# The value tiles of an mLSTM projection: 640 tokens with x stationary, and a written order of the first loads

## The chip, the core and the metric

The kernel runs on one core of one Trainium2 chip, in one launch. The time is device time in microseconds (us), the median of several runs. The engines are named as in the profile: PE is TensorE's matmuls and PEld its weight loads, DVE is VectorE, ACT is ScalarE, POOL is GpSimd, SP is SyncE, which issues most DMAs. "L1360" is line 1360 of the kernel before.

## The reference

One step of a hybrid decoder layer on 1024 prompt tokens and 8 decode tokens, 1032 rows in all, of width 2048. RMSNorm, then one projection of every token, whose columns feed two groups of heads:

```python
(aq, ak, av, iq, ik, iw, az, mq, mk, mv, mi, mf, mo, mz) = jnp.split(h @ w_in, split_points, axis=-1)
```

- Sparse attention (8 query heads, 2 key heads): an indexer (iq, ik, iw) scores all keys, the best 256 are kept, and attention runs over these. The decode tokens do the same over a paged cache of 4096 positions.
- An mLSTM with 4 heads (mq, mk of 128 a head, **mv of 256 a head**, gates mi, mf), run over the prompt in chunks, with its matrix state C returned.

Both are gated (az, mo, mz), joined, multiplied with w_out and added to x; a last RMSNorm follows. Outputs are y for prompt and sample, the new keys and values, and the mLSTM states. The change bears on `mv`, 1024 of the projection's columns, and on the first 70 us.

## The kernel before, in words

**Number format.** Every matmul operand is split in two: H, its rounded part, and L, the rest. A product is H·xH + H·xL + L·xH, three matmuls. x times the norm's weight is held in SBUF as `xH[k]` and `xL[k]`, 16 k-tiles of 128 rows x 1032 tokens. The norm's 1/rms is a factor per token, applied when a result leaves PSUM.

**The projection** is 61 tiles `t` of 128 columns. Weights are stationary, tokens move in three chunks of 344 (two of 388, from token 256 on, for the indexer's queries), and the result has columns on partitions and tokens along the free axis. `proj` (L1363) runs a tile in 4 quarters of 4 k-tiles; per quarter one DMA of 256 KB brings the raw weights (`wload`, `wsplit`, L190 to L220), ACT casts them to `wH` (L213) and DVE subtracts to get `wL` (L214). There are 2 raw buffers and 3 of H and L each. `mm` issues the matmuls (L1360). `evac` multiplies with `rstd`, tokens along the free axis, on DVE (L333), and writes the result to SBUF or by DMA to a scratch tensor in HBM. Tile order: misc (0), iq (1 to 8), ak and av (9 to 12), aq (13 to 20), mq, mk, mv (21 to 36, **mv is 29 to 36**), gates mo, mz (37 to 52), az (53 to 60).

**PSUM** has 8 banks: `pj0` to `pj2` for the projection, and five of a rotating `bank` for the rest.

**The work beside the projection.** The projection is the bed into which all else is laid. Two `Lane`s hold lists of `Job`s (from L1313): generators that do a piece of work and yield its weight. After each quarter, `lane.step(now)` lets each lane run as many pieces as the job's due tile asks for. Lane 0 has gates, index (indexer scores and a bit search for the 256th best), att, ml (the mLSTM); lane 1 has dscore (gathers from the paged cache and scores of the decode tokens), dsel, datt and dml. `gates`, `index` and `dscore` start with tile 9. A scheduler then orders each engine's queue by priority; `high_priority()` marks loads and evacuations, and `pin` fixes instructions in the order in which they are written.

**mLSTM.** `evac` writes q, k and v of the mLSTM to `mlS` (`mlS<-ev` in the DMA groups). `job_ml` later fetches one chunk of 128 tokens and one pair of heads per step, 16 steps, and in its preparation (L818 to L835) transposes the four 128 x 128 blocks of v on PE (L826) so that tokens lie on partitions, and copies them out of PSUM to `aH` (L833).

**The start.** `xbegin` (L269) loads the first k-tile of x in three pieces with the first weights; `xload` (L294) loads each further k-tile whole (516 KB), splits it on ACT (L265) and DVE (L266), squares it on ACT and adds the squares into `acc` on DVE. Tiles 0, 1 and 2 run together while x arrives, in seven PSUM banks (three for tile 0, two for each of the others). After their last matmul `row_rstd` (L233) sums `acc` over the partitions on PE (L239), takes the power -1/2 on POOL (L248), and turns the result with nine transposes (L255) and copies on DVE (L257) into `rstd`; then the three tiles are evacuated.

**The output projection** uses two forms: 392 tokens with weights stationary (L1487), and 640 tokens with the activations stationary and 512 columns of weights moving (L1525).

Of the kernel before, what the change touches and what calls it, by code (L numbers as in the profile page):

```python
# [41 lines left out]
T_AK = 9  # L42
T_AV = 11
T_AQ = 13
T_MQ = 21
T_MK = 25
T_MV = 29
# [18 lines left out]
def column_order():  # L66
    off = np.cumsum([0, 1024, 256, 256, 1024, 64, 16, 1024, 512, 512, 1024, 4, 4, 1024, 1024])
    aq, ak, av, iq, ik, iw, az, mq, mk, mv, mi, mf, mo, mz = off[:14]
    misc = np.concatenate([np.arange(ik, ik + 64), np.arange(iw, iw + 16),
                           np.arange(mi, mi + 4), np.arange(mf, mf + 4)])  # L70
    cols = [iq + np.arange(1024), ak + np.arange(256), av + np.arange(256),
            aq + np.arange(1024), mq + np.arange(512), mk + np.arange(512), mv + np.arange(1024)]
# [3 lines left out]
    return misc, np.concatenate(cols)  # L76
# [22 lines left out]
class Lane:  # L99
# [26 lines left out]
    def step(self, now):  # L126
        self.now = now
        self.debt -= 1.0
# [12 lines left out]
def body(tc, A, stop=None):  # L141
# [32 lines left out]
    cntp = ear.tile([128, 2, NB], F32, name="cntp")  # L174
    mhalf = fix.tile([128, 1], F32, name="mhalf")
# [57 lines left out]
    def row_rstd(accs, out, n, pool):  # L233
        m = (n + 127) // 128
        p = bank()
        for c in range(m):
            w = min(128, n - c * 128)
            for x, acc in enumerate(accs):
                PE.matmul(p[:w, c:c + 1], acc[:, c * 128:c * 128 + w], onesf[:, 0:1],  # L239
                          start=(x == 0), stop=(x == len(accs) - 1))  # L240
        r = pool.tile([128, 16], F32, name="rr", bufs=1)
        V.memset(r, 1.0)
        f = n // 128
        V.tensor_scalar(r[:, :f], p[:, :f], 1.0 / D, EPS, OP.mult, OP.add)
        if f < m:
            w = n - f * 128
            V.tensor_scalar(r[:w, f:m], p[:w, f:m], 1.0 / D, EPS, OP.mult, OP.add)
        G.tensor_tensor(r[:, :m], r[:, :m], mhalf.to_broadcast([128, m]), OP.pow)  # L248
        yield
        for c4 in range(0, m, 4):  # L250
            p = bank()
            n4 = min(512, n - c4 * 128)
            for c in range(c4, min(m, c4 + 4)):
                w = min(128, n - c * 128)
                PE.transpose(p[:, (c - c4) * 128:(c - c4) * 128 + w], r[:w, c:c + 1].to_broadcast([w, 128]),  # L255
                             ident[:w, :w])
            V.tensor_copy(out[:, c4 * 128:c4 * 128 + n4], p[:, :n4])  # L257
            yield
# [10 lines left out]
    def xbegin():  # L269
# [21 lines left out]
        pin(SC.activation(acc, xr, AF.Square))  # L291
        return [w[:2] for w in ws]

    def xload(k):  # L294
# [5 lines left out]
        sq = x0.tile([128, R], F32, name="sq", bufs=2)  # L300
        SC.activation(sq, xr, AF.Square)
        V.tensor_tensor(acc, acc, sq, OP.add)
# [3 lines left out]
    def chunks(t):  # L306
        return CHQ if T_IQ <= t < T_AK else CH

# [10 lines left out]
    def evac(t, ps, cols, pool=None, norms=None):  # L319
# [3 lines left out]
        for c, (c0, cn) in enumerate(chs):  # L323
            if full is not None:
                e = full[:cols, c0:c0 + cn]
            elif t < T_AK:
# [3 lines left out]
            if T_MK <= t < T_MV:  # L330
# [8 lines left out]
            elif t < T_AK:  # L339
# [23 lines left out]
            elif t < T_G:  # L363
                j = t - T_MQ
                hp, slot = ((j // 2, j % 2), (j // 2 - 2, 2 + j % 2), (j // 4 - 2, 4 + j % 4))[min(j // 4, 2)]
# [175 lines left out]
    def job_att():  # L541
        early.close()
# [235 lines left out]
    def job_ml():  # L778
        gT = mlc["gT"]
        with tc.tile_pool(name="ml", bufs=2) as pm:  # L780
# [37 lines left out]
            def prep(c, h0, qk, vT, dk, d, qt):  # L818
# [5 lines left out]
                pv = bank().rearrange("p (a b) -> p a b", a=2)  # L824
                for x in range(4):
                    PE.transpose(pv[:, x // 2, (x % 2) * 128:(x % 2) * 128 + 128], vT[:, x, :], ident)  # L826
# [100 lines left out]
    def job_dscore():  # L927
        with tc.tile_pool(name="ds", bufs=2, side="right") as pd:
# [29 lines left out]
            for b in range(NB):  # L958
                bd = pd.tile([128, 4, 8, 16], F32, name="bd")
                pin(V.tensor_tensor(bd, iqr[:, :, :, b].unsqueeze(2).to_broadcast([128, 4, 8, 16]),  # L960
                                    g8.unsqueeze(1).unsqueeze(3).to_broadcast([128, 4, 8, 16]), OP.mult))
                ps = bank()
                for c in range(4):
                    fetch(b * 4 + c + 2)
                    yield 4
# [340 lines left out]
    def ix_weight(blocks):  # L1306
# [5 lines left out]

    lanes = [Lane([Job("gates", T_AK, T_AK + 1.5, 8500, job_gates),  # L1313
                   Job("index", T_AK, 35.5, 3000 + sum(map(ix_weight, groups)), lambda: job_index(groups)),
                   Job("att", T_MQ, 47.75, 2 * 2 * sum(2 * (1 + (i + 1) * 0.5) for i in range(8)) + 6, job_att, att_free),
                   Job("ml", T_G + 11.25, T_PRE, 38, job_ml)]),
             Lane([Job("dscore", T_AK, 18, 16 + 128 + 2, job_dscore),
                   Job("dsel", T_AK, 34, 2000 + 31 * 1700 + 10000 + 16 * 2800 + 2000, job_dsel),
# [33 lines left out]
    def wsrc(t, q):  # L1352
        return A["wm"][q] if t == 0 else A["wa"][t - 1, q]

    def mm(ps, cols, t, q, c, H, L):
        c0, cn = chunks(t)[c]
        for k in range(4):
            kk = q * 4 + k
            for w_, x_, z in ((H, xH, 0), (H, xL, 1), (L, xH, 2)):
                PE.matmul(ps[:cols, :cn], w_[:, k, :cols], x_[kk][:, c0:c0 + cn],  # L1360
                          start=(kk == 0 and z == 0), stop=(kk == 15 and z == 2))

    def proj(ts, hook=None):  # L1363
# [7 lines left out]
        for q in range(4):  # L1371
            ws = []
            for x, t in enumerate(ts):
                cols = NMISC if t == 0 else 128
                with tc.high_priority():
# [4 lines left out]
                    elif x:  # L1380
                        ws.append(wsplit(wsrc(t, q), cols, x0, 2, 4, q == 1))
                    else:
                        ws.append(wsplit(wsrc(t, q), cols, wst, 2, 3))
            for x, t in enumerate(ts):
# [12 lines left out]

    pend = []
    mids = []

    def xhook(q, ws):
        if q:
            ws.append(wsplit(wsrc(0, q), NMISC, wst, 2, 3, q == 1))
        else:
            ws += xbegin()
        for k in range(max(1, q * 4), q * 4 + 4):
            xload(k)
            if k == 2:
                SY.dma_start(cst, A["cst"][:, :NCST])
                with tc.tile_pool(name="c0", bufs=1) as c0p:  # L1410
                    ctmp = c0p.tile([128, 256], F32, name="ctmp")
                    SY.dma_start(ctmp, A["cst"][:, C_TRI:C_TRI + 256])
                    V.tensor_copy(trib, ctmp[:, :128])
                    V.tensor_copy(cmask[:, 128:256], ctmp[:, 128:256])

    pss = proj((0, 1, 2), xhook)
    with tc.high_priority():
        for _ in row_rstd([acc], rstd, R, x0):
            pass
    x0ctx.close()  # L1420
    with tc.tile_pool(name="mp", bufs=1) as mp, tc.tile_pool(name="iqp", bufs=1) as iqp:
# [5 lines left out]
        for t in range(3, T_AK):  # L1427
# [3 lines left out]
            if t == 3:  # L1431
                index_weights(misc)
    for t in range(T_AK, NT):
# [24 lines left out]
    def finish(ys, accs):  # L1458
        c0, cn = CB[0]
        rs = pb.tile([128, cn], F32, name="rs", bufs=1)  # L1460
        rr = row_rstd(accs, rs, cn, pb)
# [127 lines left out]
def layout(x_prompt, x_sample, cache_k, cache_v, cache_idx_k, state_C, state_n, state_m, page_table,  # L1589
# [6 lines left out]
    misc, cols = column_order()  # L1596
    a["wm"] = w[:, misc].reshape(4, 4, 128, NMISC).transpose(0, 2, 1, 3)
    a["wa"] = w[:, cols].reshape(4, 4, 128, NT - 1, 128).transpose(3, 0, 2, 1, 4)
# [60 lines left out]
```

## Time and profile before

| | |
|---|---|
| median of 3 runs | 2039.86 us (2039.61 to 2044.28) |
| the profiled execution | 2039.7 us, of which its span is 2037.9 |
| granted clock of PE, mean | 0.998 |
| busy: PE, PEld | 99%, 96% of the span |
| busy: DVE, ACT, POOL | 58%, 38%, 12% |
| DMA | 257.08 MB, 126 GB/s on the mean |
| loads of projection weights after tile 0 (`wraw<-in_wa_dram`) | 238 of 256 KB |
| writes of mq, mk, mv (`mlS<-ev`) | 48 of 128 KB and smaller ones |

A row of a group reads: line, engine, operation, out<-in, shape, how many, then busy us in all and mean ns of one, then idle time of the engine just before it with what ended that. A row of the timeline reads start, duration, engine, line, operation and count, in brackets the idle time before and its releaser. A row of the chain reads start, length and the run of work. A window row reads window, length, busy us (instructions) of PE, PEld, DVE, ACT and POOL, PE's granted clock, the DMA share and GB/s. Matmuls are pipelined: one starts before the records let the one before end.

### The profile page before, as it was taken

The numbers are of one execution on the slowest core, as the hardware profiler recorded it, in microseconds if no ns is written. First come the engines' busy times: TensorE is split into PE (matmuls) and PEld (weight loads), VectorE is DVE, ScalarE is ACT, GpSimd is POOL, SyncE is SP. The second block draws the span as 40 slices with busy tenths as digits, with TensorE's granted clock in tenths as the row PEclk, the third lists the DMA queues.
The fourth block names the chain that finished last, engine by engine and source line by source line (L and its number), as shares of the span: only waits on it lengthen the run. The fifth ranks groups of instructions, "written<-read, shape, count | busy, mean of one in ns | idle before, by whom it ended". The sixth has DMA issues, their size and how long they took to land.

```text
span 2037.9 us, 34353 instructions
## 1 busy us (share of the span) xinstructions
PE 2022.5 (99%) x12678; PEld 1950.9 (96%) x12678; DVE 1182.2 (58%) x2956; ACT 777.7 (38%) x1631; POOL 235.2 (12%) x294
## 2 busy tenths in 40 slices
PE   9999999999999999999999999999999999999998
PEld 8999999999999999999999999999999999998886
DVE  8333367665696876878354554446677466664331
ACT  8121234233631446312255554534444344433222
POOL 0000111100000000023211011012222211111110
PEclk9999999999999999999999999999999999999999
DMA  7444533322222212244323332146675558566212
GB/s 247 106 112 125 154 111 114 100 84 63 76 75 70 75 56 63 64 142 154 120 70 92 110 95 86 48 131 197 207 217 176 152 184 314 174 223 221 81 49 103
DMA packets 203669, 257.08 MB, mean 126 GB/s; under 512 B 39685, under 2 KB 130885, under 8 KB 203501
## 3 DMA queue, kind: packets, MB, share of 16 engines
q1 hardware_dynamic: 198253, 240.82, 38.1%
q0 software_dynamic: 4096, 12.59, 2.0%
q8 instruction: 99, 1.62, 0.3%
q10 hardware_dynamic: 1152, 1.49, 0.2%
q14 instruction: 69, 0.57, 0.1%
HBM read 195.00 MB, written 59.82 MB: 125 GB/s over the span
## 4 chain that ended last, share of the span: by engine, by line
PE 96%; issue 1%; DVE 1%; ACT 1%; DMA 1%; SPq 0%; POOLq 0%; POOL 0%; DVEq 0%
PE pj L1360 62%; PE bank L1487 7%; PE bank L1525 6%; PE pj L1525 4%; PE bank L461 3%; PE bank L656 3%; PE bank L605 3%; PE bank L647 2%; PE bank L968 1%; PE bank L1360 1%; DMA xr<-in_xT_dram 1%; PE bank L845 1%; PE bank L851 1%; PE bank L847 1%; PE bank L1084 0%
## 5 line engine op out<-in xcount | busy, mean ns | idle before, releaser
L1360 PE MATMUL pj<-xH,wH 128*128 128x344 f32 (+2 forms) x2736 | 881.4, 324 | 4.0 <-ACT xH L265 2.1
L1360 PE MATMUL pj<-xH,wL 128*128 128x344 f32 (+2 forms) x2736 | 882.0, 323 | 0.0
L1360 PE MATMUL pj<-xL,wH 128*128 128x344 f32 (+2 forms) x2736 | 881.3, 322 | 0.2 <-DVE xL L266 0.2
L1360 PEld LDWEIGHTS pj<-xH,wH 128*128 128x128 f32 (+1 forms) x2736 | 513.1, 188 | 7.8 <-ACT xH L265 3.4
L1360 PEld LDWEIGHTS pj<-xL,wH 128*128 128x128 f32 (+1 forms) x2736 | 512.8, 187 | 3.1 <-DVE xL L266 1.0
L1360 PEld LDWEIGHTS pj<-xH,wL 128*128 128x128 f32 (+1 forms) x2736 | 513.3, 188 | 2.1
L213 ACT CAST wH<-wraw 128x512 fp32r<-128x512 f32 (+2 forms) x375 | 228.4, 613 | 640.4 <-PE pj L1360 422.7
L214 DVE TENSOR_TENSOR wL<-wraw,wH 128x512 fp32r<-128x512 f32 (+2 forms) x375 | 263.0, 707 | 330.6 <-ACT wH L213 302.4
L510 ACT ACTIVATE eq<-eq 128x512 bf16<-128x512 bf16 (+2 forms) x93 | 78.4, 843 | 114.4 <-DVE eq L509 111.8
L333 DVE TENSOR_TENSOR ev<-pj,rstd 128x344 f32<-128x344 f32 x144 | 73.9, 514 | 70.6 <-PE pj L1360 58.8
L463 ACT ACTIVATE rl<-bank 128x512 f32<-128x512 f32 (+2 forms) x160 | 78.7, 522 | 89.0 <-PE bank L461 63.3
L466 DVE SCALAR_TENSOR_TENSOR s<-rl,wiN,s 128x512 f32<-128x512 f32 (+2 forms) x150 | 94.8, 655 | 27.1 <-ACT rl L463 24.3
L652 DVE TENSOR_TENSOR ptL<-bank,ptH 128x512 fp32r<-128x512 f32 (+1 forms) x80 | 50.5, 635 | 66.9 <-ACT ptH L651 66.2
L1487 PE MATMUL bank<-mL,wH 128*128 128x392 f32 x256 | 87.2, 341 | 0.0
L1487 PE MATMUL bank<-mH,wL 128*128 128x392 f32 x256 | 86.9, 341 | 0.0
L1487 PE MATMUL bank<-mH,wH 128*128 128x392 f32 x256 | 86.6, 341 | 0.0
L461 PE MATMUL bank<-ki,qi 128*128 128x512 f32 (+2 forms) x320 | 76.3, 358 | 0.0
L1525 PE MATMUL bank<-wH,mH 128*128 128x512 f32 x192 | 75.4, 393 | 0.0
L1525 PE MATMUL bank<-wH,mL 128*128 128x512 f32 x192 | 75.2, 392 | 0.0
L1525 PE MATMUL bank<-wL,mH 128*128 128x512 f32 x192 | 75.2, 392 | 0.0
L336 POOL COPY dec<-ev 128x8 f32<-128x8 f32 x28 | 14.1, 505 | 514.9 <-DVE ev L333 262.1
L651 ACT CAST ptH<-bank 128x512 fp32r<-128x512 f32 (+1 forms) x80 | 42.9, 540 | 66.9 <-PE bank L647 63.2
(389 smaller groups left out, 2858.1 us busy)
## 6 DMA issues: line engine op xcount, KB each, us to landing
wraw<-in_wa_dram SPq DMA_DIRECT2D x238, 256.0 KB
wraw<-in_wo_dram SPq DMA_DIRECT2D x64, 256.0 KB
wraw<-in_wt_dram SPq DMA_DIRECT2D x64, 256.0 KB
gateS<-ev SPq DMA_DIRECT2D x72, 172.0 KB
qkv<-mlS SPq DMA_DIRECT2D x16, 512.0 KB
xr<-in_xT_dram SPq DMA_DIRECT2D x15, 516.0 KB
qi<-qS SPq DMA_DIRECT2D x24, 256.0 KB
mlS<-ev SPq DMA_DIRECT2D x48, 128.0 KB
```

Source lines behind the costliest of these rows:

```text
L213: a = SC.copy(H[:, s, :cols], raw[:, s, :cols])
L214: return a, V.tensor_tensor(L[:, s, :cols], raw[:, s, :cols], H[:, s, :cols].bitcast(F32), OP.subtract)
L333: V.tensor_tensor(e, ps[c][:cols, :cn], rstd[:cols, c0:c0 + cn], OP.mult)
L461: PE.matmul(p[:, :cn], qi[:, h % 4, :], ki[x][:, c0:c0 + cn], start=(x == 0), stop=(x == 1))
L463: SC.activation(r[:, :cn], p[:, :cn], AF.Relu)
L466: v = V.scalar_tensor_tensor(s[:, c0:c0 + cn], r[:, :cn], wv, s[:, c0:c0 + cn], OP.mult, OP.add)
L510: SC.activation(junk2[:, :W1], junk2[:, :W1], AF.Copy, accum_out=cnt[:, 1:2])
L605: PE.matmul(p[:, :cn], a_[:, h, :], b_[:, c0:c0 + cn], start=(z == 0), stop=(z == 2))
L656: PE.matmul(oT[:, :256], a_[:, k2 + kk, :], b_[:, ks_], start=(k2 + kk == 0 and z == 0), stop=(k2 + kk == i and z == 2))
L1360: PE.matmul(ps[:cols, :cn], w_[:, k, :cols], x_[kk][:, c0:c0 + cn], start=(kk == 0 and z == 0), stop=(kk == 15 and z == 2))
L1487: PE.matmul(p, w_[:, k, :], x_, start=(n == 0), stop=(n == 47))
L1525: PE.matmul(p, x_[:, bs], w_.rearrange("p a b -> p (a b)"), start=(n == 0 and z == 0), stop=(n == KT - 1 and z == 2))
```

## The change

1. **Place.** The eight mv tiles come right after the indexer's queries, as tiles 9 to 16; ak, av, aq, mq and mk each move back by eight places. Gates and az stay. `gates`, `index` and `dscore` start at tile 9 as before; their due tiles are the same.
2. **Form.** A new `vproj` replaces `proj` for these tiles. For each half of 512 columns (two heads) it runs two parts: three blocks of 128 tokens and one column block of 392 tokens; then two blocks and three column blocks. In a block x is stationary, 512 columns of weights move, and the result has tokens on partitions (tokens 0 to 639). In a column block weights are stationary and tokens 640 to 1031 move, as before. All four or five banks of a part grow together over the 16 k-tiles, so one weight piece (one k-tile x 512 columns, 256 KB) is loaded per k-tile and part: 64 pieces instead of 32. A third raw buffer is added. `lane.step` takes a fraction of a quarter after each k-tile, 32 quarters in all as before.
3. **Evacuation.** Blocks leave on ACT, scaled by a per-partition 1/rms (`rtok`, the untransposed result of `row_rstd`, now kept), in pieces of 256 columns; column blocks on DVE in two pieces. Writes to `mlS`: 36 in place of 56 for mv.
4. **mLSTM.** For chunks 0 to 4 `job_ml` uses v as it comes; the four transposes remain for chunks 5 to 7.
5. **Start.** The second k-tile of x also comes in three pieces with pinned splits; all x loads are pinned, each quarter's behind that quarter's weights; two constant loads move from behind k-tile 2 to behind k-tile 9; sums and transposes of `row_rstd` are issued between the matmuls of tile 2 in the last quarter, not behind them.
6. **Dscore.** The block matrix `bd` has one buffer, not three, and is made two quarters after a batch begins.

The core of the diff:

```diff
+    def vproj():
+        pv = vctx.enter_context(tc.tile_pool(name="pv", bufs=1))
+        c0, cn = CB[0]
+        now = 4.0 * T_MV
+        parts = (((0, 1, 2), (0,)), ((3, 4), (1, 2, 3)))
+        spans = [len(bs) * 512 + len(js) * cn for bs, js in parts]
+        for g in range(2):
+            for (bs, js), span in zip(parts, spans):
+                ps = [bank() if x is None else psj.tile([128, 512], F32, name=f"pj{x}")
+                      for x in (None, 0, 1, 2, None)[:len(bs) + len(js)]]
+                for n in range(KT):
+                    with tc.high_priority():
+                        raw = (pv if n % 3 == 2 else wst).tile([128, 4, 128], F32, name="wraw", bufs=1 if n % 3 == 2 else 2)
+                        H, L = (wst.tile([128, 4, 128], F32R, name="w" + y, bufs=3) for y in "HL")
+                        SY.dma_start(raw, A["wv"][g, n].rearrange("p (a b) -> p a b", a=4))
+                        SC.copy(H, raw)
+                        V.tensor_tensor(L, raw, H.bitcast(F32), OP.subtract)
+                    prods = ((H, xH[n]), (H, xL[n]), (L, xH[n]))
+                    for p, b in zip(ps, bs):
+                        for z, (w_, x_) in enumerate(prods):
+                            PE.matmul(p, x_[:, b * 128:b * 128 + 128], w_.rearrange("p a b -> p (a b)"),
+                                      start=(n == 0 and z == 0), stop=(n == KT - 1 and z == 2))
+                    for p, j in zip(ps[len(bs):], js):
+                        for z, (w_, x_) in enumerate(prods):
+                            PE.matmul(p[:, :cn], w_[:, j, :], x_[:, c0:R],
+                                      start=(n == 0 and z == 0), stop=(n == KT - 1 and z == 2))
+                    amount = 16.0 * span / (sum(spans) * KT)
+                    for lane in lanes:
+                        lane.step(now, amount)
+                    now += amount
+                with tc.high_priority():
+                    for p, b in zip(ps, bs):
+                        for y in range(2):
+                            e = evp.tile([128, CN], F32, name="ev")
+                            SC.activation(e[:, :256], p[:, y * 256:y * 256 + 256], AF.Copy, scale=rtok[:, b:b + 1])
+                            SY.dma_start(mlS[b, :, g, 4 + 2 * y:6 + 2 * y, :],
+                                         e[:, :256].rearrange("p (a b) -> p a b", a=2))
+                    for p, j in zip(ps[len(bs):], js):
+                        for t0, t1 in ((c0, c0 + 256), (c0 + 256, R)):
+                            e = evp.tile([128, CN], F32, name="ev")
+                            V.tensor_tensor(e[:, :t1 - t0], p[:, t0 - c0:t1 - c0], rstd[:, t0:t1], OP.mult)
...
-                pv = bank().rearrange("p (a b) -> p a b", a=2)
-                for x in range(4):
-                    PE.transpose(pv[:, x // 2, (x % 2) * 128:(x % 2) * 128 + 128], vT[:, x, :], ident)
+                if c < NT0 // 128:
+                    pv = vT.rearrange("p (h x) t -> p h (x t)", h=2)
+                else:
+                    pv = bank().rearrange("p (a b) -> p a b", a=2)
+                    for x in range(4):
+                        PE.transpose(pv[:, x // 2, (x % 2) * 128:(x % 2) * 128 + 128], vT[:, x, :], ident)
...
+        x1 = x0.tile([128, R], F32, name="xr")
+        for c in range(3):
+            pin(SY.dma_start(x1[:, cs[c]], A["xT"][1, :, cs[c]]))
+        for c in range(3):
+            a, v = xsplit(1, x1, cs[c])
+            pin(a)
+            pin(v)
...
     def xload(k):
         xr = x0.tile([128, R], F32, name="xr")
-        dma = SY.dma_start(xr, A["xT"][k])
-        if k < 4:
-            pin(dma)
+        pin(SY.dma_start(xr, A["xT"][k]))
...
             for x, t in enumerate(ts):
                 cols = NMISC if t == 0 else 128
                 H, L = ws[x]
                 for c in range(len(pss[x])):
-                    mm(pss[x][c], cols, t, q, c, H, L)
+                    step = lambda: next(norm, None)
+                    between = {(2, 0): {0: step}, (2, 1): {0: step, 2: step}}.get((x, c)) if hook and q == 3 else None
+                    mm(pss[x][c], cols, t, q, c, H, L, between or {})
...
+    norm = row_rstd([acc], rstd, R, rtok, True)
     pss = proj((0, 1, 2), xhook)
     with tc.high_priority():
-        for _ in row_rstd([acc], rstd, R, x0):
+        for _ in norm:
             pass
```

More of the change, by code (lines that the diff above doesn't have):

```diff
@@ L41 @@
 T_IQ = 1
[L42 to L47, printed above, removed]
+T_MV = 9
+T_AK = 17
+T_AV = 19
+T_AQ = 21
+T_MQ = 29
+T_MK = 33
 T_G = 37
@@ L124, in _ready, with step @@
         return bool(self.jobs) and self.jobs[0].start * 4 <= self.now and all(f() for f in self.jobs[0].conds)
-    def step(self, now):
+    def step(self, now, amount=1.0):
         self.now = now
-        self.debt -= 1.0
+        self.debt -= amount
         while self.debt < 0:
@@ L541, in job_att @@
     def job_att():
+        vctx.close()
         early.close()
@@ L1358, in mm @@
             kk = q * 4 + k
+            if k in between:
+                with tc.high_priority():
+                    between[k]()
             for w_, x_, z in ((H, xH, 0), (H, xL, 1), (L, xH, 2)):
[L1360 to L1361 removed]
+                m = PE.matmul(ps[:cols, :cn], w_[:, k, :cols], x_[kk][:, c0:c0 + cn],
+                              start=(kk == 0 and z == 0), stop=(kk == 15 and z == 2))
+                if k in between and z == 0:
+                    pin(m)
     def proj(ts, hook=None):
@@ L1426, in body @@
                 evac(t, pss[t], 128, iqp)
-        for t in range(3, T_AK):
+        for t in range(3, T_MV):
             pss = proj((t,))
```

102 lines of the change are left out of this document (63 added, 39 removed).

## The prediction

> **What bounds the kernel now.** First the page: who is busy, and what the chain of work that ended last is made of.
>
> ```profile
> span 2037.9 us, 34353 instructions
> PE 2022.5 (99%) x12678; PEld 1950.9 (96%) x12678; DVE 1182.2 (58%) x2956; ACT 777.7 (38%) x1631; POOL 235.2 (12%) x294
> PE 96%; issue 1%; DVE 1%; ACT 1%; DMA 1%; SPq 0%; POOLq 0%; POOL 0%; DVEq 0%
> L1360 PE MATMUL pj<-xH,wH 128*128 128x344 f32 (+2 forms) x2736 | 881.4, 324 | 4.0 <-ACT xH L265 2.1
> L1360 PE MATMUL pj<-xH,wL 128*128 128x344 f32 (+2 forms) x2736 | 882.0, 323 | 0.0
> L1360 PE MATMUL pj<-xL,wH 128*128 128x344 f32 (+2 forms) x2736 | 881.3, 322 | 0.2 <-DVE xL L266 0.2
> ...
> L1525 PE MATMUL bank<-wH,mH 128*128 128x512 f32 x192 | 75.4, 393 | 0.0
> ```
>
> TensorE (PE) is busy 99% of the span and carries 96% of the chain. But the three L1360 groups alone sum to 881.4 + 882.0 + 881.3 = 2644.7 us, more than the span: matmuls overlap in the records, so a mean of 324 ns is not the price of one. The price is the distance from one start to the next, read from unbroken pieces of the chain of work that ended last (start, length, what):
>
> ```profile
> 300.51 5.66 PE pj L1360 x36
> ...
> 1668.79 137.54 PE bank L1487 x768
> ...
> 1853.33 2.10 PE pj L1525 x9
> ...
> 1974.41 43.95 PE bank L1525 x192
> ```
>
> A matmul of 344 columns costs 5.66/36 = 0.1572 us, one of 392 columns (L1487, weights stationary) 137.54/768 = 0.1791, one of 512 columns (L1525, activations stationary) between 43.95/192 = 0.2289 and 2.10/9 = 0.2333. The last two are the two forms that the change brings to the v projection, so their rows price it. Then the waits of PE (line, releaser: us in all, times, longest):
>
> ```profile
> PE pj L1360 <- ACT xH L265: 2.1, 2, 1.4
> PE pj L1360 <- DVE ev L333: 1.2, 1, 1.2
> PE bank L162 <- DVE cmask L157: 1.0, 1, 1.0
> PE bank L255 <- DVE rstd L257: 0.8, 1, 0.8
> PE bank L1360 <- ACT wH L213: 0.8, 1, 0.8
> PE pj L1360 <- DVE mfull L333: 0.7, 1, 0.7
> PE pj L1360 <- DVE xL L266: 0.2, 1, 0.2
> ```
>
> All of it is 6.8 us. So a gain can only be PE work that goes, or a share of these 6.8 us, most of which lies in the first 70 us; a loss is any wait that PE does not have now.
>
> **The v matmuls (a).** Removed: 8 tiles x 16 k-tiles x 3 products x 3 chunks = 1152 x 0.1572 = 181.1 us. Added: 2 halves x 5 blocks x 16 x 3 = 480 of 512 columns, and 2 x 4 x 16 x 3 = 384 of 392 columns. With 0.230 for the first, inside the two rows and nearer to that with 192 of them, 110.4 + 68.8 = 179.2 us: **-1.9**. With 0.2289 it is 178.7 (-2.4), with 0.2333 it is 180.8 (-0.3).
>
> The Trainium skill, page "TensorE: Matmul & The Clock Gate", section "Back-to-back issue gap", gives a warm gap of N/2.4 + 2.5 ns; by an estimate from that the sum would be 1152 x 145.8 = 168.0 against 480 x 215.8 + 384 x 165.8 = 167.3 us, so -0.7 instead of -1.9. The rows above lie 11 to 15 ns over it, so the rows decide; they make a fixed part per matmul larger, which favours the longer matmuls.
>
> **The transposes (b).** The mLSTM preparation turns four blocks of v per step (L826), 64 in all; for chunks 0 to 4, ten of its 16 steps, v now comes with tokens on partitions.
>
> ```profile
> 1403.46 0.44 PE bank L826 x4
> ```
>
> ```profile
> 1330.00:1600.00 270.00, 270.00 (x1813) 267.96 (x1812) 174.97 (x582) 115.77 (x274) 60.86 (x110) 1.00 0.58 181
> ```
>
> The second row (window, length, busy us of PE, PEld, DVE, ACT, POOL, clock, DMA share, GB/s) says that PE is full in that stage, so 10 x 0.44 = **-4.4** counts whole. ACT's copy (L833) then needs no PE result, only the DMA, which is fetched a step ahead; a miss there is covered by projection matmuls. Bounds -4.4 and -3.4.
>
> **The start (c).** PE rows of the timeline, with idle time before and releaser in brackets:
>
> ```profile
> 9.12 0.34 PE L1360 MATMUL bank<-xH,wL 128*128 128x388 f32 x1
> 10.87 0.39 PE L1360 MATMUL pj<-xH,wH 128*88 128x344 f32 x1 [1.41 <-ACT xH L265]
> ...
> 26.09 0.63 PE L1360 MATMUL pj<-xH,wH 128*88 128x344 f32 x3
> 27.47 0.45 PE L1360 MATMUL bank<-xH,wH 128*128 128x388 f32 x1 [0.75 <-ACT wH L213]
> ...
> 67.78 0.60 PE L255 MATMUL bank<-cst,rr 128*128 128x128 f32 x4
> 69.17 0.22 PE L255 MATMUL bank<-cst,rr 8*128 8x8 f32 x1 [0.79 <-DVE rstd L257]
> 70.06 0.45 PE L1360 MATMUL pj<-xH,wH 128*128 128x388 f32 x1 [0.68 <-DVE mfull L333]
> ```
>
> Distance less the work's own spacing: 10.87 - 9.12 - 0.18 = 1.57 (PE waits for all of x1), 27.47 - 26.09 - 3 x 0.157 = 0.91 (weights of tile 1 behind x loads), 69.17 - 67.78 - 4 x 0.11 = 0.95 (the rstd copy between transposes), 70.06 - 69.17 - 0.04 = 0.85 (evacuation of the first tile): 4.3 us. The change splits x1 in three pieces, puts each quarter's weights ahead of its x loads on SP's queue, and steps the rstd chain between the matmuls of tile 2, whose last 24, in two chunks, then still feed PE. I let 0.4 stay at x1/x2 and 0.5 at the rstd chain, whose long link is POOL's power:
>
> ```profile
> 60.73 1.81 POOL L248 TENSOR_TENSOR rr<-rr,mhalf 128x9 f32<-128x9 f32 x1 [60.30 <-DVE rr L247]
> ```
>
> A chunk of 12 matmuls at no more than 0.179 (388 columns against 392), 2.1 us, covers it with nothing over for the links around it. So **-3.4**. Bounds: -4.3, and +1 if the pinned order (three extra DMAs and splits; constants now queued behind x9; weights ahead of x) makes x late instead: in the first 70 us DVE and DMA are no longer far from full.
>
> ```profile
> 0.00:70.00 70.00, 64.45 (x377) 60.26 (x377) 49.11 (x66) 42.71 (x54) 2.00 (x5) 1.00 0.57 184
> 190.00:380.00 190.00, 190.00 (x1249) 188.18 (x1248) 113.39 (x304) 65.83 (x158) 30.04 (x34) 1.00 0.40 126
> ```
>
> **New waits in the v stage (d).** The stage of some 180 us now stands where the second row measures the stage around tile 9 on, beside the index and dscore jobs. It loads 64 weight pieces where 8 tiles loaded 32. One piece feeds PE for 9 x 0.230 + 3 x 0.179 = 2.61 us in the first part and 6 x 0.230 + 9 x 0.179 = 2.99 us in the second, against 5.66 before. Each needs, in in-order queues shared with the jobs:
>
> ```profile
> L214 DVE TENSOR_TENSOR wL<-wraw,wH 128x512 fp32r<-128x512 f32 x28 | 19.3, 689 | 25.2 <-ACT wH L213 20.1 <-DMA akS<-ev 4.9
> L213 ACT CAST wH<-wraw 128x512 fp32r<-128x512 f32 x28 | 17.3, 619 | 78.0 <-PE pj L1360 74.0 <-issue 4.1
> ...
> L333 DVE TENSOR_TENSOR ev<-pj,rstd 128x344 f32<-128x344 f32 x21 | 10.8, 516 | 18.1 <-PE pj L1360 15.3 <-issue 2.6
> ...
> L960 DVE TENSOR_TENSOR bd<-iqr,g 128x512 f32<-128x512 f32 x7 | 8.1, 1158 | 0.0
> ...
> L971 DVE SCALAR_TENSOR_TENSOR tm<-bank,wib 128x512 f32<-128x512 f32 x6 | 7.0, 1164 | 0.0
> ```
>
> By these, 36 more pieces (64 against the window's 28) add 36 x 0.689 = 24.8 to DVE and 36 x 0.619 = 22.3 to ACT; 21 scalings of 10.8 go from DVE, and 16 of 256 columns come there, 20 to ACT, each some 0.4 by its fewer columns (L333's 0.516 for 344). DVE goes from 113.4 to about 134 of 190, ACT from 65.8 to about 96, and DMA from 126 by 9.4 MB/190 us = 50 to 176 GB/s, no more than the 184 that the first 70 us show. On average all fits; what matters is order within a queue. The tightest place is the bit search, whose DVE compares wait for ACT's accumulating passes, round by round:
>
> ```profile
> 306.29 0.16 DVE L518 COPY_PREDICATED im<-im 128x2 int32<-128x2 int32 x1
> ...
> 309.22 0.17 DVE L518 COPY_PREDICATED im<-im 128x2 int32<-128x2 int32 x1
> ...
> 325.59 0.17 DVE L518 COPY_PREDICATED im<-im 128x2 int32<-128x2 int32 x1
> ...
> 327.90 0.16 DVE L518 COPY_PREDICATED im<-im 128x2 int32<-128x2 int32 x1
> ```
>
> A round with a subtract costs 2.31 us where the subtract falls into the wait for ACT (second pair) and 2.93 where it stands ahead of the compares (first pair). Beside the search, PE does dscore's matmuls:
>
> ```profile
> 299.62 0.89 PE bank L968 x8
> ```
>
> The search's 31 rounds fall on some 27 pieces, and dscore's L960 and L971 (2.3 us, with a reduction some 3, for each of its 8 batches, 7 of them here, over 64 pieces) add 0.33 a piece. So the supply takes 2.31 x 31/27 + 0.33 = 2.98 us per piece. PE takes 2.61 to 2.99 of v matmuls and, with 256 dscore matmuls at 0.89/8 = 0.11 over 64 pieces, 0.4 more: 3.0 to 3.4. That is just enough, with three buffers for lookahead. Dscore's L960 and L971 and the scalings at the four part ends (a bank is needed again after 1 to 2 us) can each hold a piece up for about a microsecond. I take **+1.5**, about one such microsecond at the worst of each kind; bounds 0 and +8 (0.125 us at every piece).
>
> **At no cost:** 32 more weight issues and 20 fewer mlS writes on SP's queue, which is far from full at DMA share 0.40; the gathers and the dec copies on POOL (8 as before; 30 us busy of 190). The later places of attention's tiles: its first matmul stands at 1000 us, far behind both. The index job has 3 or 4 banks in place of 5; its matmuls wait for ACT and DVE anyway.
>
> Sum, against the profiled execution's own 2039.7 us (span 2037.9 and 1.8 around it, 0.2 under the median of the runs): -1.9 - 4.4 - 3.4 + 1.5 = -8.2, so **2031.5 us**, some 0.2 more by the median.
>
> **The rivals.**
> - *The start gains nothing.* The first loads set the pace anyway (184 GB/s in the row of the first 70 us, DVE 49 of 70 us), and each wait removed comes back at the next x. For it: the two waits for x are on DMA and DVE work whose amount stays. Against: 1.8 of the 4.3 us are the rstd chain, into which the change puts matmuls that stand ahead of it now. 2039.7 - 1.9 - 4.4 + 1.5 = 2034.9.
> - *The subtract does not fit into the wait in the search.* Rounds of 2.93 in place of 2.31: half of the time the supply is 3.7 us against 3.2, so 27 x 0.5 = 13.5 us in place of 1.5: 2043.5. For it: the first pair of rows is that case, and now there is a subtract in nearly every round.
> - *Weights are late at every piece (slower).* Place: PE's first matmul of each k-tile waits for wH or wL; price 0.4 to 0.5 us at each of 64, 26 to 32 us in place of 1.5: 2056 to 2062. It decides from 8.2 + 1.5 = 9.7 us in all, 0.15 us a piece (no gain), and from 0.25 a piece it is slower by more than 0.3%. For it: per piece PE has half the time, and DVE's queue is full 134 of 190 us. Against: average shares, and L213's 78.0 us idle, of which 74.0 end with PE setting a buffer free: ACT waits for PE now, not PE for ACT.
> - *Busy time is the price.* 1152 x 0.323 = 372 against 480 x 0.393 and 384 of between 0.323 and 0.393 (0.34 by their columns), 319, would be -53: 1987. Against: the sum of 2644.7 us over the span.
>
> **How the numbers follow.** Forecast 0.55, with a range of its own of 2028 to 2034; start without gain 0.14; search 0.12; weights late 0.17; busy time 0.02. The range leaves out the last two: 2026 (all of the good bounds: -2.4 - 4.4 - 4.3 + 0 = -11.1, and 2 for a piece of another wait) to 2044.5 (the search case and one more). 0.3%, 6.1 us, is about what a measurement of this kernel tells from no change: faster is under 2033.8, same up to 2046. Faster 0.53 + 0.02 and a little of the second case, 0.57; slower 0.17; the rest 0.26.
>
> **What would show it.** In the chain after, pieces of the x-stationary line at 0.229 to 0.233 us a matmul and of the other at 0.179; the group of transposes with 24 in place of 64; the first matmul of tile 3 some 3.4 us ahead of 70.06; PE's waits with few entries on the v cast and subtract lines, under 0.1 us a piece. The prediction is wrong if these entries reach 10 us, if x waits in the first 60 us sum to as much as before, or if the mLSTM stage does not shorten by 4 us.

## The result, and the profile after

| kernel | median, us | before beside it | ratio, 95% interval |
|---|---|---|---|
| changed | 2037.41 (2035.77 to 2040.34, 22 runs) | 2039.91 (22 runs) | 0.9986 (0.998 to 0.9991) |

The change gains 2.5 us, 0.14%: clear of noise, under the 0.3% set as a bound, and a third of the 8.2 us forecast. The profiled execution of the changed kernel took 2039.68 us (span 2037.9), 2.3 us over its median; one of its losses is larger than usual, as the first experiment's text says below.

The page after. PE is as full as before, although it has 328 matmuls fewer:

```profile
span 2037.9 us, 33872 instructions
...
PE 2021.8 (99%) x12350; PEld 1928.4 (95%) x12350; DVE 1198.2 (59%) x2982; ACT 805.6 (40%) x1685; POOL 233.0 (11%) x294
...
PE 96%; DMA 2%; issue 1%; DVE 1%; SPq 0%; ACT 0%; POOL 0%; POOLq 0%; DVEq 0%; ACTq 0%
```

Two per cent of the chain is now DMA. The waits of PE (L1385 is the projection's matmul, L349 the scaling out of PSUM):

```profile
PE pj L1385 <- DVE ev L349: 3.2, 1, 3.2
PE bank L585 <- DMA pP<-avS: 1.3, 2, 1.1
PE bank L162 <- DVE cmask L157: 1.0, 1, 1.0
PE pj L1385 <- ACT xH L269: 0.7, 1, 0.7
PE bank L1306 <- DMA kv<-in_cv_dram,idxs: 0.5, 1, 0.5
PE pj L1385 <- DVE mfull L349: 0.5, 1, 0.5
PE pj L1385 <- DVE ev L347: 0.3, 1, 0.3
```

The start's waits have shrunk, and no line of the v stage (L1447 to L1472) stands here. The largest is one wait of 3.2 us for an ordinary scaling. To place the gains and losses, I count the matmuls of the old form (144 a tile) and read when each tile's first one starts. Gates and az have the same numbers in both kernels:

| first matmul of tile | before | after | difference |
|---|---|---|---|
| 3 | 70.06 | 67.54 | -2.5 |
| 37 (all values done) | 916.57 | 911.96 | -4.6 |
| 49 | 1335.60 | 1335.02 | -0.6 |
| 50 | 1359.26 | 1363.28 | +4.0 |
| 55 | 1508.96 | 1509.02 | +0.1 |
| 60 | 1645.99 | 1646.06 | +0.1 |

So the three places that the change aims at gain 2.5 (start), 2.1 (values) and 4.0 us (tiles 50 to 55, the transposes): 8.6 together. Between tiles 37 and 50, in work that the change does not touch, 8.6 us are lost again, 4.0 of them up to tile 49 and 4.6 from tile 49 to 50. This is the place of the 4.6, on PE of the changed kernel:

```profile
1336.83 0.32 PE L1385 MATMUL pj<-xH,wL 128*128 128x344 f32 x1
1340.33 0.43 PE L1385 MATMUL pj<-xH,wH 128*128 128x344 f32 x1 [3.17 <-DVE ev L349]
...
1341.28 0.49 PE L1385 MATMUL pj<-xL,wH 128*128 128x344 f32 x1
1341.57 0.49 PE L1385 MATMUL pj<-xH,wL 128*128 128x344 f32 x1
```

The first two rows are one wait of 3.3 us beyond the spacing. The last two are 0.29 us apart, not 0.157; the window row has PE's granted clock at 0.50 (after the five busy times):

```profile
1341.00:1344.00 3.00, 3.00 (x11) 2.60 (x11) 1.90 (x6) 2.93 (x6) 2.05 (x3) 0.50 0.01 3
```

A standstill of 3.3 us is thus followed by some 3 us at half clock, which cost 1.5 to 2 us more. The Trainium skill, page "TensorE: Matmul & The Clock Gate", section "What's actually happening", has the clock fall to half after an idle window of about 3.4 us; this trace agrees roughly, with 3.17 us of idle, and the last section has waits of this kernel after which the clock behaved otherwise. Now the DVE queue behind which PE stood, and the same scaling's reader on POOL:

```profile
1333.24 0.51 DVE L349 TENSOR_TENSOR ev<-pj,rstd 128x344 f32<-128x344 f32 x1
1334.22 0.43 DVE L832 TENSOR_TENSOR qt<-qkv,rb 128x256 f32<-128x256 f32 x1 [0.47 <-DMA rb<-rowS]
1339.39 0.23 DVE L1135 TENSOR_TENSOR gi<-gi,bb 128x64 f32<-128x64 f32 x1 [4.75 <-DMA bb<-in_bg_dram]
...
1339.76 0.51 DVE L349 TENSOR_TENSOR ev<-pj,rstd 128x344 f32<-128x344 f32 x1
```

```profile
1340.69 0.93 POOL L406 TENSOR_TENSOR ev<-ev 128x344 f32<-128x344 f32 x1 [14.39 <-DMA ev<-gateS]
```

DVE scales the first chunk of tile 48, then reaches an addition of the decode mLSTM job (L1135), which waits 4.75 us for a small load. The second scaling stands behind it, and PE needs that bank for tile 49. Before, the same addition at the same kind of wait has no scaling behind it:

```profile
1350.08 0.23 DVE L1113 TENSOR_TENSOR gi<-gi,bb 128x64 f32<-128x64 f32 x1 [3.02 <-DMA bb<-in_bg_dram]
```

There the mLSTM jobs' first loads (`qkv`, `gi`) leave SP after two of the evacuation's three gate loads, the second of which is the first row here (SP's queue before: start, duration, line):

```profile
1334.10 0.46 SPq L389 DMA_DIRECT2D ev<-gateS  x1
...
1336.50 0.42 SPq L797 DMA_DIRECT2D qkv<-mlS  x1
...
1340.38 0.98 SPq L1103 DMA_DIRECT2D gi<-miscS  x1
```

In the changed kernel they leave ahead of all three:

```profile
1326.30 0.42 SPq L814 DMA_DIRECT2D qkv<-mlS  x1
...
1328.19 0.52 SPq L1125 DMA_DIRECT2D gi<-miscS  x1
...
1330.30 0.58 SPq L1128 DMA_DIRECT2D bb<-in_bg_dram  x1
...
1333.72 0.91 SPq L405 DMA_DIRECT2D ev<-gateS  x2
```

### The profile page after: what moved, and what is told of

Same layout as the page of the kernel before. It is cut to its first block, busy times and chain, and to the rows that moved or that the text cites. A ratio compares the mean times of both kernels' runs of the same rounds, so it can differ in the third digit from the quotient of the medians.

```text
span 2037.9 us, 33872 instructions
## 1 busy us (share of the span) xinstructions
PE 2021.8 (99%) x12350; PEld 1928.4 (95%) x12350; DVE 1198.2 (59%) x2982; ACT 805.6 (40%) x1685; POOL 233.0 (11%) x294
## 4 chain that ended last, share of the span: by engine, by line
PE 96%; DMA 2%; issue 1%; DVE 1%; SPq 0%; ACT 0%; POOL 0%; POOLq 0%; DVEq 0%; ACTq 0%
PE pj L1385 53%; PE bank L1571 7%; PE bank L1609 6%; PE pj L1609 4%; PE pj L1452 3%; PE bank L477 3%; PE bank L673 3%; PE pj L1456 3%; PE bank L622 3%; PE bank L1452 2%; PE bank L1385 2%; PE bank L664 2%; PE bank L990 1%; PE bank L1456 1%; PE bank L865 1%
## 5 line engine op out<-in xcount | busy, mean ns | idle before, releaser
L1385 PE MATMUL pj<-xH,wH 128*128 128x344 f32 (+2 forms) x2352 | 760.3, 325 | 4.7 <-DVE ev L349 3.2
L1385 PE MATMUL pj<-xL,wH 128*128 128x344 f32 (+2 forms) x2352 | 761.1, 324 | 0.0
L1385 PE MATMUL pj<-xH,wL 128*128 128x344 f32 (+2 forms) x2352 | 759.4, 323 | 0.0
L1385 PEld LDWEIGHTS pj<-xH,wH 128*128 128x128 f32 (+1 forms) x2352 | 442.0, 188 | 8.3 <-DVE ev L349 3.9
L1385 PEld LDWEIGHTS pj<-xH,wL 128*128 128x128 f32 (+1 forms) x2352 | 442.0, 188 | 2.2
L1385 PEld LDWEIGHTS pj<-xL,wH 128*128 128x128 f32 (+1 forms) x2352 | 441.9, 188 | 2.1 <-DVE xL L270 0.4
L215 DVE TENSOR_TENSOR wL<-wraw,wH 128x512 fp32r<-128x512 f32 (+2 forms) x343 | 243.8, 718 | 324.8 <-ACT wH L214 316.0
L214 ACT CAST wH<-wraw 128x512 fp32r<-128x512 f32 (+2 forms) x343 | 209.2, 613 | 565.5 <-PE pj L1385 366.8
L482 DVE SCALAR_TENSOR_TENSOR s<-rl,wiN,s 128x512 f32<-128x512 f32 (+2 forms) x150 | 95.1, 655 | 30.1 <-ACT rl L479 28.3
L349 DVE TENSOR_TENSOR ev<-pj,rstd 128x344 f32<-128x344 f32 x120 | 61.5, 513 | 44.0 <-PE pj L1385 37.5
L1448 DVE TENSOR_TENSOR wL<-wraw,wH 128x512 fp32r<-128x512 f32 x64 | 44.1, 689 | 43.1 <-ACT wH L1447 36.0
L1447 ACT CAST wH<-wraw 128x512 fp32r<-128x512 f32 x64 | 39.4, 617 | 75.2 <-PE pj L1456 34.1
```

The source lines that it names most:

```text
L214: a = SC.copy(H[:, s, :cols], raw[:, s, :cols])
L215: return a, V.tensor_tensor(L[:, s, :cols], raw[:, s, :cols], H[:, s, :cols].bitcast(F32), OP.subtract)
L349: V.tensor_tensor(e, ps[c][:cols, :cn], rstd[:cols, c0:c0 + cn], OP.mult)
L482: v = V.scalar_tensor_tensor(s[:, c0:c0 + cn], r[:, :cn], wv, s[:, c0:c0 + cn], OP.mult, OP.add)
L1385: m = PE.matmul(ps[:cols, :cn], w_[:, k, :cols], x_[kk][:, c0:c0 + cn], start=(kk == 0 and z == 0), stop=(kk == 15 and z == 2))
```

## The experiments

The first theory (A): the aimed-at gains are real, and a fixed order of the queues near tile 49 eats them. Its rivals: the stall is the accident of one execution; or the new form itself costs what it gains.

**The changed kernel once more**, no edit.

> The changed kernel once more, as it is, for a second profile. Theory A (queue order): the loss lies in unchanged work between tiles 38 and 50 and is fixed by the order of the queues, so this profile again shows DVE's addition of the gate biases (decode mLSTM job) waiting 4 to 5 us for its DMA with a projection scaling behind it, PE idle 2 to 3.4 us for that scaling, and the clock below 1 for some 3 us after it; time 2037 to 2040 us. Theory B (chance of one execution): the wait is shorter than 1 us here or PE does not stand still behind it, and the time is the same 2037.4 us, so the stall of the first profile explains nothing of the median.

2038.85 us, before beside it 2041.03, ratio 0.9994 (0.9985 to 1.0003). The profile has the addition waiting again, PE standing 3.9 us beyond the spacing before tile 49's second chunk, and the clock at 0.66 over 1335 to 1345:

```profile
1337.36 0.23 DVE L1135 TENSOR_TENSOR gi<-gi,bb 128x64 f32<-128x64 f32 x1 [4.62 <-DMA bb<-in_bg_dram]
```

The stall near tile 49 comes again. Between tiles 37 and 49 this execution loses 1.1 us, not 4.0. The 2.9 us on top lie in tile 39, with late gathers and a slow clock near 970 us; they come and go with the execution. Tile 39 takes 32.5 us in before, 36.4 in the first profile of the changed kernel and 33.3 in the second; of the later runs' profiles, two have it long, that of the buffer alone (35.9) and that of the old form (35.3).

**The addition later.**

```diff
-            for _ in range(4):
+            for _ in range(8):
                 yield 2000
             pin(V.tensor_tensor(gi, gi, bb.unsqueeze(3)...
```

> The changed kernel with the addition of the gate biases issued after eight yields of the decode mLSTM job, not four; nothing else differs. Theory A: the loads have landed when DVE comes to the addition, the idle of 3.2 us and the slower clock behind it (1.7 us) go: 3 to 5 us less than the changed kernel, 2032.5 to 2034.5 us. Theory B: no more than 1 us less, 2036.5 to 2037.5 us.

2037.56 us, ratio 0.9985 (0.9976 to 0.9994) beside 2041.03: 1.3 us less than the changed kernel run beside it, so theory A failed here as it was put. Its DVE says why. The addition is gone, but the third scaling waits in its place, with POOL as releaser:

```profile
1339.56 0.52 DVE L349 TENSOR_TENSOR ev<-pj,rstd 128x344 f32<-128x344 f32 x1 [6.45 <-POOL ev L406]
```

A scaling writes one of six `ev` buffers. Each chunk of a mz tile takes three: the result, its gate, and a gate product that is loaded. POOL cannot free any until the load `ev<-gateS` lands. That load stands behind the mLSTM jobs' first loads. PE's stall is still 3.3 us. So there are two waits in one place, and each is enough (theory C).

**The start alone and the old start.** Before with the change's part 5 only, and the changed kernel without it.

> The kernel before with the new start alone (x1 in pieces, pinned x loads behind the weights, constants behind k-tile 9, the rstd chain between the matmuls of tile 2); values projected as before. The order of DVE's queue around the gate biases is that of before, with no scaling behind the addition. Theory A: first matmul of tile 3 at 67.5 us in place of 70.1, and these 2.5 us are kept to the end: 2037.4 us. Theory B (gains of the start are given back by later waits): tile 3 at 67.5, but the end within 1 us of before, 2039 to 2040 us.

2038.06 us, ratio 0.9989 (0.998 to 0.9998): tile 3 starts at 67.03 us. By the ratio 2.2 us reach the end, as theory A has it. The profile, an execution 1.0 us over the median, keeps less of it: tile 3 starts 3.0 us earlier than before, tile 37 2.0, tile 38 only 0.4, and the span is 0.7 us shorter. PE waits 2.4 us for a scaling ahead of tile 37, where it waited 1.2 in before, and behind that its clock is 0.66 from 915 to 920 us:

```profile
914.61 0.40 PE L1379 MATMUL pj<-xH,wH 128*128 128x344 f32 x1 [2.37 <-DVE ev L349]
```

So a later wait can take back part of the start, as theory B has it; how often it does, one profile doesn't tell.

> The changed kernel with the start of before. Theory A: first matmul of tile 3 at 70.1 us; the v stage gains some 2 us and the mLSTM stage 4; the order of DVE's queue around the gate biases is that of the changed kernel, so the stall is there; 2.5 us more than the changed kernel: 2039.9 us, no faster than before. Theory B: the end is that of the changed kernel within 1 us, 2036.5 to 2038.5 us.

2040.91 us, ratio 1.0001 (0.9992 to 1.001). Without the start the rest of the change is worth nothing that these runs could measure, and the stall is there (3.4 us beyond the spacing at 1336.5). Tile 3 starts at 68.95, so this start is also 1.1 us earlier than before's; I did not look into why.

**Both cures.** The kernel of the later addition, with a buffer of its own for the third scaling once the mLSTM job runs.

```diff
+            elif c == 2 and xev:
+                e = xev[0].tile([128, CN], F32, name="ex")
             else:
                 e = evp.tile([128, CN], F32, name="ev")
...
+        xev.append(xectx.enter_context(tc.tile_pool(name="evx", bufs=1, side="right")))
         with tc.tile_pool(name="ml", bufs=2) as pm:
```

> The kernel of dml8 (addition issued later) with one buffer more for the third scaling of a tile, from the start of the mLSTM job on. Theory C (the ring of six ev buffers is held by the gating on POOL, whose gate load stands behind the mLSTM jobs' first loads): the third scaling near 1332 us needs no returned buffer, PE's idle of 3.3 us before tile 49's next chunk is under 1 us, and so is any slower clock behind it: 3 to 5 us less than dml8, 2032.5 to 2034.5 us. Theory D (the loads themselves are late and any consumer is held): ACT or PE waits elsewhere for the same loads, and the time is within 1.5 us of dml8, 2036 to 2038 us.

**2031.78 us in 5 runs, ratio 0.9957 (0.9943 to 0.997)** beside 2041.02: by the ratios 6 to 7.5 us less than the changed kernel in its two sets of runs. Theory C holds, and the gain is a little over the 3 to 5 us that it was given. The waits of PE in it:

```profile
PE bank L162 <- DVE cmask L157: 1.0, 1, 1.0
PE pj L1390 <- DVE ev L349: 1.0, 1, 1.0
PE pj L1390 <- ACT xH L269: 0.7, 1, 0.7
PE bank L587 <- DMA pP<-avS: 0.6, 1, 0.6
PE pj L1390 <- DVE mfull L351: 0.5, 1, 0.5
```

The stall is gone, although POOL waits as long as ever. The third scaling no longer needs POOL's buffer:

```profile
1332.60 0.50 DVE L351 TENSOR_TENSOR ex<-pj,rstd 128x344 f32<-128x344 f32 x1
```

```profile
1338.33 0.93 POOL L408 TENSOR_TENSOR ev<-ev 128x344 f32<-128x344 f32 x1 [14.97 <-DMA ev<-gateS]
```

From tile 49 to tile 50 it takes 23.1 us, where the changed kernel took 28.3 and 29.6 in its two profiles and before 23.7.

**The buffer alone**, with the addition where the changed kernel has it.

> The changed kernel with the extra buffer for the third scaling, but the gate biases added where the changed kernel adds them. Theory C2 (two waits in one place, each enough to hold PE): DVE's addition still waits 4 to 5 us for its load with the second scaling behind it, PE stands 3 us there, and the time is that of the changed kernel within 1.5 us, 2036.5 to 2039.5 us. Rival (the buffer alone is the cause, the addition only looked like one): 2031 to 2034 us.

2039.6 us, ratio 0.9988 (0.9979 to 0.9997) beside 2041.87. As theory C2 has it: the addition still waits, and the buffer brings nothing by itself. PE stands there twice, 2.6 and 1.5 us beyond the spacing.

```profile
1339.41 0.23 DVE L1138 TENSOR_TENSOR gi<-gi,bb 128x64 f32<-128x64 f32 x1 [4.19 <-DMA bb<-in_bg_dram]
```

**Both cures in the kernel before.**

> The kernel before with both cures, the later addition and the extra buffer. Theory C: before has no stall at that place, so the cures bring nothing: 2040 to 2041 us, within 1 us of before run beside it. Rival (the cures make any kernel faster, and the loss was not the change's): 3 us or more less.

2040.92 us, ratio 0.9997 (0.9988 to 1.0006). The cures are worth something only where the change put the stall.

**What holds the gate loads.** The kernel of the later addition, the five small loads of the decode mLSTM job (`gi` twice, `bb`, `sn`, `m0`) issued by ACT; the first of the five edits:

```diff
-            SY.dma_start(gi[:, 0], miscS[80:84, S:R].partition_broadcast(128))
+            SC.dma_start(gi[:, 0], miscS[80:84, S:R].partition_broadcast(128))
```

> The kernel of dml8 with the five small loads of the decode mLSTM job issued on ACT's queue in place of SP's; the ring of ev buffers as in the changed kernel. Theory E (the gate loads wait behind the small packets of the broadcasts): the gate loads land within 3 to 4 us of their issue, POOL's gating starts near 1335 us in place of 1338 to 1340, PE's idle falls under 1 us, 2031.5 to 2034 us. Theory F (they wait for the 512 KB and 256 KB fetches, or for bandwidth): POOL's gating starts no earlier and the time is that of dml8 within 1.5 us, 2036 to 2038.5 us.

2036.37 us, ratio 0.9975 (0.9964 to 0.9985), inside theory F's range. The loads, though, land as fast as theory E has it:

```profile
1335.59 0.91 SPq L405 DMA_DIRECT2D ev<-gateS  x2
```

```profile
1338.55 0.92 POOL L406 TENSOR_TENSOR ev<-ev 128x344 f32<-128x344 f32 x1 [13.90 <-DMA ev<-gateS]
```

```profile
1334.15 0.43 DVE L832 TENSOR_TENSOR qt<-qkv,rb 128x256 f32<-128x256 f32 x1 [10.04 <-DMA rb<-rowS]
```

The gating starts 3.0 us after the loads' issue, against 7.0 in the changed kernel (1333.72 to 1340.69) and 6.9 in the kernel of the later addition (1331.71 to 1338.62). But the loads are issued 3.9 us later than in the latter, so the gating starts no earlier. DVE now stands 10 us at the mLSTM's `rb` load, with two scalings behind it, and PE is idle for 1.9 us there. The order of loads has changed with the edit, so this run doesn't separate small packets from order alone; that the small broadcasts ahead on the same queue made most of the 7 us is likely, not shown. The Trainium skill, page "DMA: Bandwidth & Descriptors", section "Queues, rings and completion order", says that SP and ACT have rings of their own, whose descriptors are consumed in ring order; the shorter delay fits that.

**The transposes kept.** The 40 transposes issued into a bank that nobody reads, so that their PE time is there and the data path is the new one.

> The changed kernel with the 40 transposes of v blocks issued as before into a PSUM bank that nobody reads; the copies read v directly. Theory A: PE is full in the mLSTM stage, so the end is 4.0 to 4.4 us later than the changed kernel, 2041 to 2043 us, and the 4 us show between the starts of tiles 50 and 55. Rival: the transposes fit into waits of that stage, and the end is less than 1.5 us later.

2040.8 us, ratio 0.9999 (0.999 to 1.0008): 2 us over the changed kernel's second run, with intervals that overlap, and just under theory A's range. The trace is sharper. From tile 50 to 55 it takes 149.8 us; changed 145.7; before 149.7. Transposes are worth 4.0 us, all of it on PE's path in that stage.

**The new place with the old form.** Values at tiles 9 to 16, weights stationary, 32 loads.

> The changed kernel with the v tiles at their new place and the new start, but in the old form: weights stationary, 344 tokens moving, 32 loads, 64 transposes. DVE's queue has the addition of the gate biases between the second and the third scaling of a tile. Theory A: against the changed kernel 2 us are lost in the v tiles and 4 in the transposes, and the stall near tile 49 stays or is replaced by one like it: 2042 to 2045 us. Rival (the new form's side effects cost what it gains): 2037 to 2039 us.

2044.32 us, ratio 1.0012 (1.0003 to 1.0021): slower than before, by 0.12%. The stall is there, 3.8 us beyond the spacing, for a scaling behind the addition:

```profile
1339.35 0.23 DVE L1135 TENSOR_TENSOR gi<-gi,bb 128x64 f32<-128x64 f32 x1 [4.30 <-DMA bb<-in_bg_dram]
```

So the new form is not needed for the stall, nor is the new start (the run with the old start has it, the start alone has no wait there). What is left is the new place or part 6, the later `bd` of dscore, which this run keeps; no run separates the two. The form with its transposes is worth 5.5 us by the second run of the changed kernel.

**Two raw buffers in the v stage.**

```diff
-                        raw = (pv if n % 3 == 2 else wst).tile([128, 4, 128], F32, name="wraw", bufs=1 if n % 3 == 2 else 2)
+                        raw = wst.tile([128, 4, 128], F32, name="wraw", bufs=2)
```

> The changed kernel with two raw weight buffers in the v stage, not three. Theory A (supply has slack; it was not the loss): PE's waits between 170 and 390 us stay under 1.5 us in all and the time within 1 us of the changed kernel. Rival (weights late): 64 pieces each wait 0.1 to 0.4 us, 6 to 25 us more.

2038.13 us, ratio 0.9985 (0.9976 to 0.9994), as the changed kernel. PE's waits from 165 to 395 us are one:

```profile
PE bank L477 <- DMA wraw<-in_wv_dram: 0.2, 1, 0.2
```

The supply of weights was never tight; even the third buffer is not needed.

## Why the prediction was wrong

**The step that failed** is the one headed "At no cost". It set "the later places of attention's tiles" to nothing because attention's first matmul stands far behind them. That only shows that no data is late. It does not show that the queues keep their order: in the changed kernel the mLSTM jobs' first loads leave at 1326 us in place of 1336, against an evacuation that stayed where it was, and the order of DVE's instructions, the same in both profiles of the changed kernel, had the addition between two scalings. (Whether the place alone does this, or part 6 has a share, stays open.) Priced from the profiles, tile 49 takes 28.3 and 29.6 us in the changed kernel and 23.1 in the cured one: 5.2 to 6.5 us, of which 3.3 to 3.9 are standstill and the rest mostly half clock. By the ratios of the medians the cures bring 6 to 7.5 us. With the term at nothing the forecast was 2031.5, a ratio of 0.996 to the 2039.7 that it started from; the cured kernel has 0.9957 (0.9943 to 0.997). That the sum comes out so well is in part luck, as two of its other terms were off in opposite ways.

**The start (c)**, -3.4: -2.5 and -2.6 in the two profiles of the changed kernel, -3.0 in the start alone. Right in kind. PE's waits fell as put (xH 2.1 to 0.7, the first evacuation 0.7 to 0.5, those on xL, wH and the rstd copy gone, 3.4 us together); 0.9 us of it came back. In the changed kernel's profile the first matmuls run slowly: those of 344 columns start 0.29 us apart up to 9.6 us, the spacing that half clock gave near 1342 us, where in before they start 0.15 apart (after, then before):

```profile
8.11 0.49 PE L1385 MATMUL pj<-xL,wH 128*88 128x344 f32 x1
8.40 0.49 PE L1385 MATMUL pj<-xH,wL 128*88 128x344 f32 x1
...
10.82 0.48 PE L1385 MATMUL pj<-xH,wH 128*88 128x344 f32 x2
```

```profile
8.28 0.32 PE L1360 MATMUL pj<-xL,wH 128*88 128x344 f32 x1
8.43 0.32 PE L1360 MATMUL pj<-xH,wL 128*88 128x344 f32 x1
```

So the first matmul on x1 starts at 10.82 us, as late as in before (10.87), though it waits for nothing: the 1.2 us put on that wait went into slow matmuls ahead of it. In the profile of the start alone these matmuls are 0.16 us apart (7.37 and 7.53), and tile 3 starts half a microsecond earlier. Whether the new start or chance brings the slow stretch, the runs don't show.

**The v matmuls (a) and their waits (d)**, -1.9 and +1.5. From tile 3 to 37 it measured -2.1, of which 0.9 is the wait ahead of tile 37 (L333, 1.2 us before; L347, 0.3 after). So -1.2 against -0.4. The size is known to about 1 us: this stretch takes 846.5 us in before, 844.4 to 846.3 in the profiles with the new form, and 847.6 with the new start alone. The spacings stand in the chain:

```profile
172.45 2.09 PE pj L1452 x9
...
286.56 2.79 PE pj L1452 x12
```

0.232 us for 512 columns, inside the bounds of 0.2289 and 0.2333 but nearer to the upper: -0.7 or so by itself in place of -1.9. The other error balanced it: no piece of weights was late. (The prediction also puts its rows at most 15 ns over the estimate of 215.8 ns for 512 columns; 0.2333 us is 17.5 over it.)

**The transposes (b)**, -4.4: -4.0, between its bounds.

**The rivals.** "Weights late at every piece" and "the subtract does not fit" are refuted: no wait on a cast or subtract in the v stage, with three buffers or with two. I had put 29 in 100 on these, and none on a stall in a stage that the change does not touch. "The start gains nothing" is refuted by the start alone. "Busy time is the price" is refuted by the time: it asked for -53.

**What stays open:** why the attention job ends some 10 us earlier (its last store leaves SP at 1323.37 us, in before at 1333.68) while tile 49 starts at the same time. The code gives attention the same due tile in both kernels, 47.75, and the mLSTM jobs the same first tile, 48.25. The difference is there from the job's first matmul on, which starts 3.8 us ahead of tile 40 in the changed kernel and 2.7 us behind its start in before. What sets that, no run shows.

## What to carry to other kernels

Moving work in a kernel whose engines are packed re-orders what you did not touch. Before costing unchanged stages at nothing, compare the order of each in-order queue, and look for an instruction that waits on a DMA with an evacuation behind it. A gain that has vanished is best looked for by the starts of equal milestones in both traces: here they showed within one table that 8.6 us were gained in three places and lost again between tiles 37 and 50. And a stall can have two causes in one place; curing either alone shows nothing, so try them together before dropping the theory.

## What was not expected of the hardware

- A load of 4 KB in all, the same 32 bytes to each partition, took 9.1 us from issue to use (`bb`, 1330.30 to 1339.39). It is issued behind larger loads and two other small ones. After a stretch at up to 388 GB/s the DMAs together move 6 to 21 GB/s from 1334.0 to 1336.6 us (GB/s of the changed kernel in slices of 0.375 us from 1325 on):

```profile
GB/s 0 0 0 34 135 109 350 355 328 306 229 191 219 328 355 355 328 377 388 374 198 65 55 29 7 6 6 6 7 21 6 19 63 88 152 275 314 305 262 145
```

- A standstill of PE can cost more than itself: the clock from 1335 to 1345 us was 0.83 in the first profile of the changed kernel, with 3.17 us of idle, and 0.66 in the second, with 3.8. The length doesn't decide alone. With the buffer alone, two waits of 2.4 and 1.4 us idle, 2.1 us of matmuls between them, left it at 1.00, and 1.94 us of idle in the run with loads on ACT's queue came with 0.83 (changed kernel, then buffer alone):

```profile
1335.00:1345.00 10.00, 6.83 (x34) 6.14 (x33) 3.11 (x10) 5.03 (x11) 3.28 (x4) 0.83 0.27 85
```

```profile
1335.00:1345.00 10.00, 6.20 (x39) 5.63 (x38) 3.43 (x11) 5.97 (x13) 3.22 (x4) 1.00 0.27 85
```

- The clock also fell with PE counted busy throughout: in the kernel before, a run of 24 matmuls of four columns is followed by 0.77 over 5 us.

```profile
970.02 2.74 PE L1284 MATMUL bank<-PT,kv 128*128 128x4 f32 x24
```

```profile
975.00:980.00 5.00, 5.00 (x30) 5.00 (x29) 0.00 (x0) 0.00 (x0) 3.65 (x5) 0.77 0.38 112
```
